# A hybrid mixer and MoE layer: expert weights laid out by groups of 128 rows, contiguous reads on TensorE, routing steps in another order

## The chip, the cores and the metric

The kernel runs on one core of a Trainium2 chip. The metric is the device time of one execution in microseconds (us). The engines are TensorE (PE, with its weight loads as PEld), VectorE (DVE), ScalarE (ACT), GpSimd (POOL) and SyncE (SP); DMA engines, 16 to a core, move data between HBM and SBUF.

## The reference

T = 512 tokens of D = 1024 features, float32. After four token mixers with a gated merge and an output projection (unchanged here) comes a mixture of experts:

```python
def hier_moe(h, wr_g, br_g, wr_e, br_e, w_gate, w_up, w_down):
    '''Top-1 expert group, then top-2 experts inside it; experts are SwiGLU MLPs.'''
    ...
    combine = jnp.sum(jax.nn.one_hot(expert_id, N_EXPERTS, dtype=f32) * top_w[..., None], axis=1)
    hid = jax.nn.silu(jnp.einsum('td,edf->etf', t, w_gate)) * jnp.einsum('td,edf->etf', t, w_up)
    hid = hid * combine.T[:, :, None].astype(hid.dtype)
    out = jnp.einsum('etf,efd->td', hid, w_down)
    ...
        h = h + hier_moe(rms_norm(h, norm2_g[l]), router_w_group[l], ...)
    return rms_norm(h, final_norm_g)
```

There are 16 experts of width 512 in 4 groups; gate and up weights are 1024 x 512 per expert, down weights 512 x 1024.

## The kernel before

The program runs, in this order, the input projection and the mixers, the merge with `w_out` (0 to 617 us with what follows), the routing and the dispatch (about 597 to 616), the 16 experts (616 to 925), and the way back with the last norm (925 to 950). A slot table gives each expert up to 128 tokens.

*Order.* PE's instructions run in the order in which the code issues them (a manual schedule); those of the other engines are ordered by a scheduler from their dependences, and each engine runs its own in order.

*Three passes.* The large matmuls are split into a high and a low part of each operand: ACT copies the high part (L119: `XH`, `nh`, `HH`), DVE subtracts to get the low one (L120: `XL`, `nl`, `HL`), and PE runs three matmuls (L123 to L125). An expert's gate, up and down products (G, U, D) each take four chunks of weights; one chunk is 128 x 1024 elements, feeds six matmuls of 512 columns, and costs one `nh` and one `nl`. `feed` issues these splits ahead into a few slots, which come free when PE has used them.

*Weight loads.* `wload` issues the loads of the expert weights on SP's queue, 1 MB each into one of 13 buffers (named `raw`, `wb`, `m`, `wbx`, `hi`, `lo`, after what lay there). Row r of a weight matrix goes to partition r // 8 for gate and up, and r // 4 for down: 8 KB in one run per partition and load. So partition p holds neighbouring rows, and whatever meets these weights in a matmul has to be read in columns of stride 8 (or 4 for the hidden layer).

*Routing*, for each block t of 128 tokens: `r_t` transposes the activations, `r_mm` (L1072) makes the logits and the norm's factor `rs`, and then DVE's top-k chain, up to `Msel` (one flag per token and expert); `r_h2` scales the activations (`h2`); `r_pos` counts on PE (L1111, L1112), builds the selection `sel` of expert 0 (L1116), and then some 17 small DVE operations of indices and weights; POOL scatters `h2` to `XE` in DRAM by those indices (L1131). `disp` (L1160) gathers expert 0's tokens by a matmul of `h2` and `sel`. The steps of the first three blocks are placed between the matmuls of `w_out`; those of t = 3 stand in a row, as the diff shows.

*Experts.* Expert 0 comes from `disp` directly. The others are loaded from `XE` by POOL's queue (`x_load`, L1272, L1275) and transposed on PE (`xt`, L1234). `h_tr` (L1247) transposes the hidden layer. In experts 0 and 15 U is computed in two halves of 256 columns (`up_halves`), with `h_half` (L1322), so that D can begin sooner. POOL makes index tables for expert 0 (L1294) which PE uses at L1385. At expert 14 POOL makes the tables for the return of experts 14 and 15 (`pT`, L1407), then writes the results of expert 13 to DRAM (L1364) and gathers the earlier results by token (L1372). DVE adds them to what PE returns (L1461, L1463).

Of the kernel before, what the change touches and what calls it, by code (L numbers as in the profile page):

```python
# [1549 lines left out]
```

## Time and profile before

| | |
|---|---|
| median of 3 runs | 951.55 us (951.45 to 951.55) |
| the profiled execution | 951.25 us, span 949.7 us, granted clock 0.99 |
| PE busy | 922.9 us, 97% |
| weight loads (PEld) | 760.1 us, 80% |
| DVE / ACT / POOL busy | 627.8 (66%) / 538.8 (57%) / 101.2 (11%) |
| DMA | 195.7 MB, 206 GB/s over the span |

The span is that of the engines' instructions in the profiled execution; the time of an execution is a little longer. Busy times are sums of records; PE's records overlap, because matmuls are pipelined. Such shares are means over all stages.

### The profile page before, as it was taken

The numbers are of one execution on the slowest core, as the hardware profiler recorded it, in microseconds if no ns is written. First come the engines' busy times: TensorE is split into PE (matmuls) and PEld (weight loads), VectorE is DVE, ScalarE is ACT, GpSimd is POOL, SyncE is SP. The second block draws the span as 40 slices with busy tenths as digits, with TensorE's granted clock in tenths as the row PEclk, the third lists the DMA queues.
The fourth block names the chain that finished last, engine by engine and source line by source line (L and its number), as shares of the span: only waits on it lengthen the run. The fifth ranks groups of instructions, "written<-read, shape, count | busy, mean of one in ns | idle before, by whom it ended". The sixth has DMA issues, their size and how long they took to land. (4 is left out here: it accounts for less than half of the span.)

```text
span 949.7 us, 13038 instructions
## 1 busy us (share of the span) xinstructions
PE 922.9 (97%) x4765; PEld 760.1 (80%) x4765; DVE 627.8 (66%) x1165; ACT 538.8 (57%) x837; POOL 101.2 (11%) x181
## 2 busy tenths in 40 slices
PE   8999999999999999999999999999999999999993
PEld 7979888777768888888888888977888888888882
DVE  6677457888773343444374515658989989999955
ACT  7436548558982232232263314247888888888853
POOL 2000000000000000000000011441110101110750
PEclk9999999999999999999999999999999999999997
DMA  8558456652124224222444437679999999999283
GB/s 246 143 147 283 164 192 222 218 182 89 45 74 129 65 90 131 89 89 89 133 132 163 172 117 288 253 231 332 357 355 397 377 369 382 393 386 380 66 163 110
DMA packets 90047, 195.73 MB, mean 206 GB/s; under 512 B 7388, under 2 KB 63784, under 8 KB 78712
## 3 DMA queue, kind: packets, MB, share of 16 engines
q1 hardware_dynamic: 62312, 153.56, 46.2%
q0 software_dynamic: 6528, 20.29, 7.6%
q10 hardware_dynamic: 21136, 20.98, 6.4%
q8 instruction: 39, 0.64, 0.3%
q14 instruction: 32, 0.26, 0.1%
HBM read 166.24 MB, written 34.60 MB: 211 GB/s over the span
## 5 line engine op out<-in xcount | busy, mean ns | idle before, releaser
L120 DVE TENSOR_TENSOR lo<-raw,hi 128x1024 fp32r<-128x1024 f32 (+3 forms) x70 | 79.0, 1132 | 129.4 <-ACT hi L119 129.1
L119 ACT ACTIVATE hi<-raw 128x1024 fp32r<-128x1024 f32 (+3 forms) x70 | 68.6, 986 | 161.0 <-PE b L124 88.0
L123 PE MATMUL b<-nh,XH 128*128 128x512 f32 (+1 forms) x272 | 109.9, 404 | 0.5 <-ACT XH L119 0.5
L125 PE MATMUL b<-nh,XL 128*128 128x512 f32 (+1 forms) x272 | 108.2, 398 | 0.0
L124 PE MATMUL b<-nl,XH 128*128 128x512 f32 (+1 forms) x272 | 108.1, 397 | 0.0
L123 PE MATMUL b<-nh,hi 128*128 128x512 f32 x256 | 100.1, 391 | 0.0
L124 PE MATMUL b<-nl,hi 128*128 128x512 f32 x256 | 99.8, 390 | 0.0
L125 PE MATMUL b<-nh,lo 128*128 128x512 f32 x256 | 99.7, 389 | 0.0
L123 PE MATMUL mm<-nh,hi 128*128 128x512 f32 x192 | 78.8, 410 | 1.1 <-DVE nl L235 1.1
L125 PE MATMUL mm<-nh,lo 128*128 128x512 f32 x192 | 75.2, 392 | 0.0
L124 PE MATMUL mm<-nl,hi 128*128 128x512 f32 x192 | 75.0, 391 | 0.0
L120 DVE TENSOR_TENSOR nl<-wb,nh 128x1024 fp32r<-128x1024 f32 x56 | 67.2, 1227 | 7.3 <-ACT nh L119 5.2
L120 DVE TENSOR_TENSOR nl<-m,nh 128x1024 fp32r<-128x1024 f32 x56 | 66.9, 1225 | 5.5 <-ACT nh L119 3.5
L120 DVE TENSOR_TENSOR nl<-raw,nh 128x1024 fp32r<-128x1024 f32 x52 | 62.2, 1225 | 7.6 <-ACT nh L119 6.1
L119 ACT ACTIVATE nh<-wb 128x1024 fp32r<-128x1024 f32 x56 | 58.8, 1062 | 13.5 <-PE b L125 8.2
L119 ACT ACTIVATE nh<-m 128x1024 fp32r<-128x1024 f32 x56 | 58.7, 1062 | 11.3 <-PE b L125 8.6
L119 ACT ACTIVATE nh<-raw 128x1024 fp32r<-128x1024 f32 x52 | 54.5, 1062 | 14.0 <-PE b L125 11.2
L125 PEld LDWEIGHTS b<-nh,XL 128*128 128x128 f32 x272 | 52.2, 192 | 12.0 <-DVE XL L120 0.4
L123 PEld LDWEIGHTS b<-nh,XH 128*128 128x128 f32 x272 | 52.4, 193 | 11.4 <-ACT XH L119 0.7
L124 PEld LDWEIGHTS b<-nl,XH 128*128 128x128 f32 x272 | 52.3, 192 | 10.8
L123 PEld LDWEIGHTS b<-nh,hi 128*128 128x128 f32 x256 | 48.0, 188 | 10.4 <-issue 0.2
L124 PEld LDWEIGHTS b<-nl,hi 128*128 128x128 f32 x256 | 48.1, 188 | 10.3 <-issue 0.2
(391 smaller groups left out, 2049.8 us busy)
## 6 DMA issues: line engine op xcount, KB each, us to landing
raw<-in_w_in_dram SPq DMA_DIRECT2D x30, 1024.0 KB, 5.5
XE<-MZ ACTq DMA_DIRECT2D x24, 512.0 KB, 3.8
wb<-in_moe_w_gate_dram SPq DMA_DIRECT2D x10, 1024.0 KB, 8.0
m<-in_moe_w_gate_dram SPq DMA_DIRECT2D x10, 1024.0 KB, 6.2
raw<-in_moe_w_up_dram SPq DMA_DIRECT2D x9, 1024.0 KB, 5.7
wb<-in_moe_w_down_dram SPq DMA_DIRECT2D x9, 1024.0 KB, 5.0
wb<-in_moe_w_up_dram SPq DMA_DIRECT2D x9, 1024.0 KB, 7.1
m<-in_moe_w_up_dram SPq DMA_DIRECT2D x9, 1024.0 KB, 8.3
```

Source lines behind the costliest of these rows:

```text
L119: A.activation(hi, src, AF.Copy)
L120: return V.tensor_tensor(lo, src, hi.bitcast(FT), op=OP.subtract)
L123: PE.matmul(o, w[0], xx[0], start=first, stop=False)
L124: PE.matmul(o, w[0], xx[1], start=False, stop=False)
L125: PE.matmul(o, w[1], xx[0], start=False, stop=last)
```

## The change

Expert weights are loaded so that partition p of group k holds row k·128 + p. Then `disp`, `xt`, `h_tr`, `h_half` and `up_halves` read contiguous columns. The routing steps are cut into smaller ones: `rs` and `h2` come earlier or behind `Msel`, `r_pos` keeps the count and `sel`, and the rest of it becomes `r_idx`, which for t = 2 and 3 is issued behind the last `Msel`. POOL's memsets go, since the first three loads of `X` are whole, and the tables `pT` move to DVE.

```diff
     def wload(ap, h):
...
-        src = ap.rearrange("(p k) f -> p (k f)", p=128)[:, h * 2048:(h + 1) * 2048]
-        n = 2048 // len(ws)
+        n, m = 2048 // len(ws), ap.shape[0] // 256 // len(ws)
+        src = ap.rearrange("(k p) f -> p k f", p=128)
         for i, w in enumerate(ws):
-            S.dma_start(w, src[:, i * n:i * n + n])
+            k = (h * len(ws) + i) * m
+            S.dma_start(w.rearrange("p (k f) -> p k f", k=m), src[:, k:k + m])
...
+        return p
+
+    def r_rs(t):
         s2 = sm("s2", 1)
         V.tensor_tensor(s2, ss2[:, t, 0:1], ss2[:, t, 1:2], op=OP.add)
+        rstd(rs2[:, t:t + 1], s2, D)
+
+    def r_top(t, p):
         r2 = rs2[:, t:t + 1]
-        rstd(r2, s2, D)
...
-        V.tensor_tensor(Msel[t], OH[:, 0], OH[:, 1], op=OP.add)
-        XS[t] = OH, ef, lg, g8, e8
-
-    def r_h2(t):
+        MS[t] = V.tensor_tensor(Msel[t], OH[:, 0], OH[:, 1], op=OP.add).ins
+        o0 = sm("o0", 1)
+        V.tensor_tensor(o0, OH[:, 0, 0:1], OH[:, 1, 0:1], op=OP.add)
+        XS[t] = OH, ef, lg, g8, e8, o0
+
+    def r_h2(t, behind=None):
         h2 = h2b[t]
-        V.scalar_tensor_tensor(h2, x1[:, t], rs2[:, t:t + 1], g2b, op0=OP.mult, op1=OP.mult)
-        XS[t] += (h2,)
...
+        with tc.issue_after(behind) if behind else ExitStack():
+            V.scalar_tensor_tensor(h2, x1[:, t], rs2[:, t:t + 1], g2b, op0=OP.mult, op1=OP.mult)
+        HH2[t] = h2
...
     def r_pos(t):
...
         sel = wop.tile([128, 128], FT, name="sel", bufs=4)
-        o0 = sm("o0", 1)
-        V.tensor_tensor(o0, OH[:, 0, 0:1], OH[:, 1, 0:1], op=OP.add)
         V.tensor_scalar(sel, slot, p[:, 0:1], o0, op0=OP.is_equal, op1=OP.mult)
+        SEL[t] = sel
+
+    def r_idx(t):
+        OH, ef, lg, g8, e8, o0 = XS[t]
+        p, h2 = PP[t], HH2[t]
         po = sm("po", 16)
...
     def disp(t, ks=range(KD)):
-        sel, h2 = XS[t]
-        hv = h2.rearrange("p (q k) -> p k q", k=KD)
+        sel, h2 = SEL[t], HH2[t]
         for k in ks:
-            PE.matmul(x0[k // 4][:, (k % 4) * 128:(k % 4 + 1) * 128], hv[:, k], sel, start=t == 0 and k % 4 == 0, stop=t == NT - 1,
+            PE.matmul(x0[k // 4][:, (k % 4) * 128:(k % 4 + 1) * 128], h2[:, k * 128:(k + 1) * 128], sel, start=t == 0 and k % 4 == 0, stop=t == NT - 1,
...
-        pend = [lambda t=t: r_t(t, 0), no, lambda t=t: r_t(t, 1), no, lambda t=t: (r_mm(t), r_h2(t)), no, no,
-                ] + ([lambda t=t: r_pos(t - 1)] if t else [])
+        pend = [lambda t=t: r_t(t, 0), no, lambda t=t: (r_t(t, 1), r_rs(t)), no,
+                lambda t=t: (r_top(t, r_mm(t)), r_h2(t, MS[t])), no, no,
+                ] + ([lambda t=t: (r_pos(t - 1), r_idx(t - 1))] if t else [])
     r_t(3, 0)
     disp(0, range(4))
     r_t(3, 1)
+    r_rs(3)
+    r_h2(3)
     disp(0, range(4, KD))
-    r_mm(3)
+    r_top(3, r_mm(3))
+    disp(1)
     r_pos(2)
-    r_h2(3)
-    disp(1)
     disp(2)
     r_pos(3)
     disp(3)
+    for t in (2, 3):
+        with tc.issue_after(MS[3]):
+            r_idx(t)
...
     def xt(X, q):
-        Xv = X.rearrange("p (q k) -> p k q", k=KD)
...
-                PE.transpose(p[:, k * 128:(k + 1) * 128], Xv[:, i * 4 + k], ident)
+                c = (i * 4 + k) * 128
+                PE.transpose(p[:, k * 128:(k + 1) * 128], X[:, c:c + 128], ident)
...
     def h_tr(H):
         p = bank()
-        Hv = H.rearrange("p (q k) -> p k q", k=4)
         for k in range(4):
-            PE.transpose(p[:, k * 128:(k + 1) * 128], Hv[:, k], ident)
+            PE.transpose(p[:, k * 128:(k + 1) * 128], H[:, k * 128:(k + 1) * 128], ident)
...
-    for X in Xt[1:]:
-        G.memset(X, 0.0)
...
-        if e == 1:
+        if e <= len(Xt):
             G.dma_start(X, XE[e * CAP:e * CAP + CAP])
...
-            if e in (0, NE - 1):
-                o, i = [v.rearrange(a, s=2, q=128) for v, a in ((H[e], "p (s q c) -> p q s c"),
-                                                                (pgu[k], "p (q s c) -> p q s c"))]
-                A.activation(o, i, AF.Silu)
-            else:
-                A.activation(H[e], pgu[k], AF.Silu)
+            A.activation(H[e], pgu[k], AF.Silu)
...
                 feed(1)
-                g.append([v.rearrange("p k (q s c) -> p k s q c", s=2, c=2) for v in ready.popleft()])
-            up_mm(p[s][:, :256], q[e], [v[:, :, s] for v in g[j]], j)
+                g.append(ready.popleft())
+            up_mm(p[s][:, :256], q[e], [v[:, :, s * 256:s * 256 + 256] for v in g[j]], j)
...
-                G.tensor_scalar(pT[:, t], slot, lz[:, a, 1, i:i + 1], lz[:, a, 0, i:i + 1], op0=OP.is_equal,
+                V.tensor_scalar(pT[:, t], slot, lz[:, a, 1, i:i + 1], lz[:, a, 0, i:i + 1], op0=OP.is_equal,
```

On PE, at the end of the routing, from the logits of t = 3 on. Before (`x_4861` and `x_4862` are the two banks of the dispatch, `Msel_4847` to `Msel_4849` the flags of t = 0 to 2):

```order
L1072 MATMUL b<-wr,lo 128x24 x8
L1111 LDWEIGHTS ones
L1111 MATMUL b<-Msel_4847,ones 128x16
L1111 LDWEIGHTS ones
L1111 MATMUL b<-Msel_4848,ones 128x16
L1112 LDWEIGHTS upper
L1112 MATMUL b<-Msel_4849,upper 128x16
L1160 MATMUL x_4861<-sel,lo 128x128 x4
L1160 MATMUL x_4862<-sel,lo 128x128 x4
```

After:

```order
L1073 MATMUL b<-wr,lo 128x24 x8
L1171 MATMUL x_4861<-sel,lo 128x128 x4
L1171 MATMUL x_4862<-sel,lo 128x128 x4
L1121 LDWEIGHTS ones
L1121 MATMUL b<-Msel_4847,ones 128x16
L1121 LDWEIGHTS ones
L1121 MATMUL b<-Msel_4848,ones 128x16
L1122 LDWEIGHTS upper
L1122 MATMUL b<-Msel_4849,upper 128x16
```

The dispatch of t = 1 now stands ahead of the counts of t = 2; nothing else on PE changes its place.

On DVE, where the logits of t = 3 are used. Before, the logits `lg` of t = 3, `sel` of t = 2, and the top-k chain of t = 3 (`MAX`, `MAX_INDEX`) among the operations of `r_pos(2)`:

```order
L1078 SCALAR_TENSOR_TENSOR lg<-b,rs_4852,br 128x24
L1139 TENSOR_TENSOR idx<-dd,sl 128x2
L1116 TENSOR_SCALAR sel<-slot,b,o_5388 128x128
L1080 MAX g_5365<-lg 128x8
L1118 COPY po<-b 128x16
L1082 MAX_INDEX gi_5367<-g_5365,lg 128x8
L1145 SCALAR_TENSOR_TENSOR wd<-ed,gs 128x1
L1120 TENSOR_TENSOR pm<-OH,po 128x32
L1084 CAST gi<-gi_5367 128x1
```

After, with `h2` of t = 3 (`lo`) as the first row:

```order
L1111 SCALAR_TENSOR_TENSOR lo<-xm,rs_4852,g2b 128x1024
L1142 TENSOR_TENSOR ix<-dd,sl 128x2
L1084 SCALAR_TENSOR_TENSOR lg<-b,rs_4852,br 128x24
L1150 TENSOR_SCALAR dd<-sl 128x2
L1124 TENSOR_SCALAR sel<-slot,b,o_5275 128x128
L1151 TENSOR_TENSOR dd<-dd,ovs 128x2
L1086 MAX g_5368<-lg 128x8
L1152 TENSOR_TENSOR idx<-dd,sl 128x2
L1088 MAX_INDEX gi_5370<-g_5368,lg 128x8
```

The chain of t = 3 is still behind `sel` of t = 2. The operations of `r_pos` (`po`, `pm`, `wd`) have left it; with those of t = 3 they are now 35 rows between `sel` of t = 3 and the first `XL`, of which these are the last:

```order
L1151 TENSOR_TENSOR dd<-dd,ovs 128x2
L1161 TENSOR_TENSOR w__5487<-w__5487,ed 128x1
L1152 TENSOR_TENSOR idx<-dd,sl 128x2
L1162 TENSOR_TENSOR ow<-OH,w__5487 128x32
L120 TENSOR_TENSOR XL_5505<-x_4861,XH_5504 128x512
L120 TENSOR_TENSOR XL_5505<-x_4862,XH_5504 128x512
```

The scatters of t = 2 and 3 take their indices `ix` from there, and `XL`, which the first matmuls of expert 0 need, is behind them.

On POOL, from the norm's factors `rs` on. Before (`XE<-hi,ix` and `XE<-lo,ix` are the scatters of t = 0 to 3, two instructions each):

```order
L208 TENSOR_TENSOR rs_4852<-ms,mh 128x1 x2
L1131 DMA XE<-hi,ix 3072x1024 x2
L208 TENSOR_TENSOR rs_4852<-ms,mh 128x1 x2
L1131 DMA XE<-lo,ix 3072x1024 x2
L1265 MEMSET lo 128x1024
L1131 DMA XE<-hi,ix 3072x1024 x2
L1131 DMA XE<-lo,ix 3072x1024 x2
L1265 MEMSET hi 128x1024
L1294 TENSOR_SCALAR lo<-slot,pcs 128x128 x8
```

After (L1307 are the index tables, L1294 before):

```order
L208 TENSOR_TENSOR rs_4852<-ms,mh 128x1 x3
L1144 DMA XE<-hi,ix 3072x1024 x2
L1307 TENSOR_SCALAR lo<-slot,pcs 128x128 x2
L208 TENSOR_TENSOR rs_4852<-ms,mh 128x1
L1307 TENSOR_SCALAR lo<-slot,pcs 128x128 x2
L1144 DMA XE<-lo,ix 3072x1024 x2
L1307 TENSOR_SCALAR lo<-slot,pcs 128x128 x4
L1144 DMA XE<-hi,ix 3072x1024 x2
L1144 DMA XE<-lo,ix 3072x1024 x2
```

The memsets are gone and the tables stand ahead of the scatters of t = 2 and 3.

## Rows read from the trace of the kernel before

**Rows 1.** The page: PE's busy time, and the largest group of `nl` (busy us, mean ns | idle before, releaser).

```profile
PE 922.9 (97%) x4765; PEld 760.1 (80%) x4765; DVE 627.8 (66%) x1165; ACT 538.8 (57%) x837; POOL 101.2 (11%) x181
...
L120 DVE TENSOR_TENSOR nl<-wb,nh 128x1024 fp32r<-128x1024 f32 x56 | 67.2, 1227 | 7.3 <-ACT nh L119 5.2
```

**Rows 2.** Busy time by stretch: the stretch and its length, then busy us (instructions) of PE, PEld, DVE, ACT and POOL, PE's granted clock, the share of the DMA engines, GB/s.

```profile
680.00:740.00 60.00, 60.00 (x283) 49.27 (x282) 55.06 (x54) 51.26 (x61) 7.04 (x26) 1.00 1.02 383
...
870.00:907.60 37.60, 37.60 (x175) 30.74 (x174) 33.46 (x32) 32.15 (x38) 21.27 (x18) 1.00 0.39 133
```

**Rows 3.** Timeline of PE around a contiguous group of 128x128 matmuls (L604), and in the dispatch: start us, length us, line, operation, tiles, count, and in brackets an idle time and what ended it.

```profile
178.21 1.95 PE L604 MATMUL mm<-w,yb 128*128 128x128 f32 x16
179.99 0.60 PE L827 MATMUL at<-ident,t 128*128 128x128 f32 x4
...
597.56 2.07 PE L1160 MATMUL x<-sel,hi 128*128 128x128 f32 x8
599.46 0.60 PE L1062 MATMUL b<-ident,xm 128*128 128x128 f32 x4
...
601.79 1.86 PE L1072 MATMUL b<-wr,lo 128*128 128x24 f32 x16
...
611.99 4.18 PE L1160 MATMUL x<-sel,lo 128*128 128x128 f32 x16 [0.45 <-DVE sel L1116]
...
616.97 0.40 PE L125 MATMUL b<-nh,XL 128*128 128x512 f32 x1
```

**Rows 4.** Groups by line and shape, whole span: busy us, mean ns | idle before.

```profile
L1160 PEld LDWEIGHTS x<-sel,lo 128*128 128x128 f32 x32 | 7.8, 335 | 0.5 <-DVE sel L1116 0.5
...
L604 PEld LDWEIGHTS mm<-w,yb 128*128 128x128 f32 x32 | 4.0, 191 | 0.2
...
L818 DVE TENSOR_SCALAR t<-t,sm 128x128 f32<-128x128 f32 x16 | 3.9, 284 | 0.2
```

**Rows 5.** Timeline of PE at the halves of experts 0 and 15: the first row of each (L123, 128x256) and the first of the down projection behind it.

```profile
626.05 0.46 PE L123 MATMUL b<-nh,XH 128*128 128x256 f32 x1
...
637.31 0.50 PE L123 MATMUL x<-nh,HH 128*128 128x512 f32 x1
...
907.66 0.39 PE L123 MATMUL b<-nh,XH 128*128 128x256 f32 x1
...
918.88 0.50 PE L123 MATMUL x<-nh,HH 128*128 128x512 f32 x1
```

**Rows 6.** Timeline of PE, contiguous matmuls of 256 columns: the first and the last of fifteen.

```profile
75.90 0.28 PE L568 MATMUL mm<-hi,nh 128*128 128x256 f32 x1
...
77.58 0.28 PE L568 MATMUL mm<-lo,nh 128*128 128x256 f32 x1
```

**Rows 7.** Timeline of PE, one `h_tr` and what follows.

```profile
661.57 0.63 PE L1247 MATMUL b<-ident,H 128*128 128x128 f32 x4
661.95 0.48 PE L123 MATMUL b<-nh,XH 128*128 128x512 f32 x1
```

**Rows 8.** Timeline of DVE in the routing of t = 2 and 3.

```profile
603.92 1.22 DVE L1116 TENSOR_SCALAR sel<-slot,b,o 128x128 f32<-128x128 f32 x1
...
605.20 0.09 DVE L1082 MATCH_VALUE_LOAD gi<-g,lg 128x8 f32 x1
...
607.25 0.16 DVE L1097 TENSOR_TENSOR Msel<-OH 128x16 bf16<-128x16 f32 x1
...
611.85 0.17 DVE L1118 COPY po<-b 128x16 f32<-128x16 f32 x1
...
613.84 0.16 DVE L1139 TENSOR_TENSOR idx<-dd,sl 128x2 int32<-128x2 f32 x1
```

**Rows 9.** Timeline of POOL: memset, tables, first load of X.

```profile
604.09 0.97 POOL L1265 MEMSET lo<- 128x1024 f32 x1
...
616.74 5.97 POOL L1294 TENSOR_SCALAR lo<-slot,pcs 128x128 f32<-128x128 f32 x4
...
625.71 0.63 POOL L1272 DMA_DIRECT2D hi<-XE  x1
```

**Rows 10.** Timeline of PE at the table matmuls.

```profile
622.10 1.06 PE L1385 MATMUL b<-ow,lo 128*128 128x16 f32 x8
624.07 0.40 PE L1385 MATMUL b<-ow,lo 128*128 128x16 f32 x2 [0.91 <-POOL lo L1294]
```

**Rows 11.** DMA issues of the page: KB each, median us from issue to landing.

```profile
m<-in_moe_w_up_dram SPq DMA_DIRECT2D x9, 1024.0 KB, 8.3
```

**Rows 12.** Timeline of POOL (return tables) and of DVE (first add of the return).

```profile
893.23 6.38 POOL L1407 TENSOR_SCALAR hi<-slot,lz 128x128 f32<-128x128 f32 x2
...
929.68 1.28 DVE L1463 TENSOR_TENSOR xm<-xm,b 128x512 f32<-128x512 f32 x2 [2.64 <-PE b L1461]
```

**Rows 13.** Busy time by stretch, columns as in rows 2: a long stretch with loads of `w_in` (runs of 1 KB) and `w_branch` (2 KB), one load of `w_branch` alone, one load of expert weights alone.

```profile
280.00:340.00 60.00, 60.00 (x268) 48.92 (x263) 21.45 (x23) 17.17 (x22) 0.00 (x0) 1.00 0.34 107
...
333.90:337.40 3.50, 3.50 (x18) 2.86 (x17) 0.32 (x1) 1.42 (x2) 0.00 (x0) 1.00 0.81 298
...
581.60:585.20 3.60, 3.60 (x22) 3.01 (x21) 2.20 (x8) 1.81 (x4) 0.55 (x1) 1.00 0.77 278
```

**Rows 14.** Timeline of SP (two loads of up weights) and of ACT (the first split of one of them).

```profile
814.29 2.60 SPq L1018 DMA_DIRECT2D m<-in_moe_w_up_dram  x2
...
849.24 1.07 ACT L119 ACTIVATE nh<-m 128x1024 fp32r<-128x1024 f32 x1
```

More of the change, by code (lines that the diff above doesn't have):

```diff
@@ L1054, in wo_mm @@
         sumsq(ss2[:, t, hf:hf + 1], xs, jk)
-    XS = {}
+    XS, MS = {}, {}
     def r_t(t, q):
@@ L1096, in r_mm @@
                         op=OP.is_equal)
-        V.tensor_tensor(Msel[t], OH[:, 0], OH[:, 1], op=OP.add)
-        XS[t] = OH, ef, lg, g8, e8
-    def r_h2(t):
+        MS[t] = V.tensor_tensor(Msel[t], OH[:, 0], OH[:, 1], op=OP.add).ins
[3 more added lines that the diff above has]
+    def r_h2(t, behind=None):
         h2 = h2b[t]
-        V.scalar_tensor_tensor(h2, x1[:, t], rs2[:, t:t + 1], g2b, op0=OP.mult, op1=OP.mult)
-        XS[t] += (h2,)
-    scat = []
+        with tc.issue_after(behind) if behind else ExitStack():
+            V.scalar_tensor_tensor(h2, x1[:, t], rs2[:, t:t + 1], g2b, op0=OP.mult, op1=OP.mult)
+        HH2[t] = h2
+    scat, HH2, SEL, PP = [], {}, {}, {}
     def r_pos(t):
-        OH, ef, lg, g8, e8, h2 = XS[t]
-        p = bank()
+        OH, ef, lg, g8, e8, o0 = XS[t]
+        p = PP[t] = bank()
         for tt in range(t):
@@ L1113, in r_pos @@
         sel = wop.tile([128, 128], FT, name="sel", bufs=4)
-        o0 = sm("o0", 1)
-        V.tensor_tensor(o0, OH[:, 0, 0:1], OH[:, 1, 0:1], op=OP.add)
         V.tensor_scalar(sel, slot, p[:, 0:1], o0, op0=OP.is_equal, op1=OP.mult)
+        SEL[t] = sel
+    def r_idx(t):
+        OH, ef, lg, g8, e8, o0 = XS[t]
+        p, h2 = PP[t], HH2[t]
         po = sm("po", 16)
@@ L1151, in r_pos @@
         V.tensor_copy(lz[:, t, 1], po[:, NE - 2:])
-        XS[t] = sel, h2
     x0 = [bank("x0", 2), bank("x0", 2)]
     def disp(t, ks=range(KD)):
-        sel, h2 = XS[t]
-        hv = h2.rearrange("p (q k) -> p k q", k=KD)
+        sel, h2 = SEL[t], HH2[t]
         for k in ks:
-            PE.matmul(x0[k // 4][:, (k % 4) * 128:(k % 4 + 1) * 128], hv[:, k], sel, start=t == 0 and k % 4 == 0, stop=t == NT - 1,
+            PE.matmul(x0[k // 4][:, (k % 4) * 128:(k % 4 + 1) * 128], h2[:, k * 128:(k + 1) * 128], sel, start=t == 0 and k % 4 == 0, stop=t == NT - 1,
                       skip_group_check=True)
@@ L1310, in run_up @@
             H[e] = Ht[e % 2]
-            if e in (0, NE - 1):
-                o, i = [v.rearrange(a, s=2, q=128) for v, a in ((H[e], "p (s q c) -> p q s c"),
-                                                                (pgu[k], "p (q s c) -> p q s c"))]
-                A.activation(o, i, AF.Silu)
-            else:
-                A.activation(H[e], pgu[k], AF.Silu)
+            A.activation(H[e], pgu[k], AF.Silu)
     def h_half(e, s):
         p = bank()
-        Hv = H[e][:, s * 256:s * 256 + 256].rearrange("p (q c) -> p c q", c=2)
         for c in range(2):
-            PE.transpose(p[:, c * 128:(c + 1) * 128], Hv[:, c], ident)
+            PE.transpose(p[:, c * 128:(c + 1) * 128], H[e][:, s * 256 + c * 128:s * 256 + c * 128 + 128], ident)
         o = [v[:, 2 * s:2 * s + 2].rearrange("p k t -> p (k t)") for v in HQ]
```

## The prediction

> **What bounds the kernel now.** I read the page's totals first: PE is busy 97% of a span of 949.7 us [rows 1]. So a gain has to come out of PE's own instructions, or out of one of its few waits. The table by stretches says who is next: from 680 to 740 us PE is busy all the time at a granted clock of 1.00 (the higher of its two levels, 2.4 GHz), DVE 92% of it, ACT 85%, and the DMA engines show a share above one [rows 2]. PE is first there, but DVE and the weight loads stand close behind it.
>
> Records of PE overlap, so I cost PE by the distance from one start to the next, not by mean durations. Read in that way the timeline shows two places where the same work is dear. Eight dispatch matmuls take 1.90 us (597.56 to 599.46), 238 ns each; sixteen contiguous ones of the same shape 1.78 us (178.21 to 179.99), 111 ns [rows 3]. The weight load of the dispatch matmul, which reads every eighth column, takes 335 ns against 191 [rows 4]. The halves of the up projection of experts 0 and 15 read two columns of every four: 48 matmuls and two transposes take 11.26 us (626.05 to 637.31), 229 ns each when 0.28 goes to the transposes [rows 5]; fifteen contiguous 256-column matmuls stand 120 ns apart (75.90 to 77.58) [rows 6]. The transposes of h_tr, though strided too, are not dear: four take 0.38 us [rows 7].
>
> **The change, part by part.** The profiled execution took 951.25 us, 0.3 below the median of the runs and 1.55 above its span; the sum goes against 951.25.
>
> *Dispatch and routing.* 64 matmuls × (238 − 111) ns is 8.1 us of PE work [rows 3]. Not all of it can arrive, because DVE's chain stands behind it. Step by step: the 16 matmuls of disp(0) ahead of r_mm(3) give 2.0 us, so r_mm(3), from 601.8 now, ends at about 601.5; its logits follow at 601.9, since h2(3), as wide as nl (1.23 us [rows 1]), is now ahead of them on DVE. disp(1) runs from 601.5 to 603.3 ahead of the counts of t=2; then comes sel(2), which took 1.22 us beside POOL's memset [rows 8, 9] and takes some 0.3 without it (the nearest form has 284 ns [rows 4]). Behind it on DVE stands the top-k chain of t=3, 2.2 us from the row at 605.20 to the end of Msel [rows 8]; so Msel(3) comes at about 606.1, while PE, having ended disp(2) at 605.6, waits. sel(3) at 606.6, disp(3) from 606.7 to 608.5; it started at 611.99 [rows 3]. What is late next is XL: 35 small operations of r_idx(2) and r_idx(3) stand ahead of it on DVE. Where they are independent one comes every 79 ns (605.20 to 607.25, 27 rows), in one chain every 142 (611.85 to 613.84, 15 rows) [rows 8]: 2.8 to 5.0 us from 606.6. With 0.7 us for XL, half as wide as nl, the first matmul that needs it starts between 610.1 and 612.3, against 616.97 [rows 3]. Gain 4.7 to 6.9. POOL's tables now run beside these operations and can stretch them as the memset stretched sel, so I take 5.3, and keep 3.5 as the lower bound.
>
> *Index tables of expert 0.* The matmuls at L1385 take 3.95 us (622.10 to 626.05), most of it in waits for POOL [rows 5, 10]. POOL began the tables at 616.74, behind the last scatter [rows 9]. Now the memsets are gone and the tables stand ahead of the scatters of t=2 and 3: done at about 613, before G0 ends at 616.8. Sixteen matmuls at 111 ns are 1.8 us: gain 2.15, at least 1. The price is that the last scatters, and so x_load(1), stand behind them; still it goes out at some 617 where it went out at 625.71 [rows 9], and if it lands as late as a weight load, in 8.3 us [rows 11], it is there before D0 starts (637.31 less 12 us).
>
> *Halves of experts 0 and 15.* 11.26 and 11.22 us [rows 5] become 48 × 120 ns and 0.3 for the transposes, 6.1: a gain of 5.2 each. But four chunks of weights are split in this time, and nl takes DVE 1.23 us a chunk [rows 1], so the chunks of D0 and D15 come later against PE than before. Half a microsecond each is given back: 4.7 + 4.7. The bounds are 5.2 each, and 3.2 if two are given back.
>
> *Transposes.* h_tr's 0.38 us for four is 95 ns each, less than the 111 of contiguous matmuls [rows 3, 7]: little is left to gain. 176 transposes × 0 to 5 ns: I take 0.4, bounds 0 and 0.9.
>
> *Return tables.* Eight 128x128 operations move to DVE: 284 ns each by the nearest row of that form, 2.3 us in all [rows 4]. DVE is busy 33.46 of 37.6 us there [rows 2], which covers them but for moments when a chunk has little lead: 0.3 lost, bounds 0 and 2.3. POOL is rid of them (they last until 899.61 [rows 12]), and the writes of Y13 and the gathers, which stand behind them, start sooner. This is needed: the adds of the return waited for PE, not for the gathers (2.64 us at 929.68 [rows 12]), but PE arrives 17 us sooner now.
>
> *Weights in 128-row groups.* A load of 1 MB is now in runs of 2 KB (gate, up) or 4 KB (down) rather than 8 KB. Lone loads: w_branch, in 2 KB runs, moves 298 GB/s, expert weights in 8 KB runs 278 [rows 13]. So no loss by these. Against that, a long stretch with runs of 1 and 2 KB gives 107 GB/s at a share of 0.34, 315 per full share, and the expert stretch 383 at 1.02, or 375 [rows 2, 13]: up to 19% longer. 1 MB at 383 GB/s is 2.7 us; six loads per expert would take 0 to 3.1 us more. The cover is the lead of the loads: one issued at 814.29 is used at 849.24 [rows 14] and lands in 8.3 [rows 11], so 27 us early. Over 13 experts that lasts up to 2.1 us each. I take a third of the upper price, 1 us each (nearer to the lone loads, which show it directly), and so nothing on the path.
>
> Sum: 5.3 + 2.15 + 4.7 + 4.7 + 0.4 − 0.3 = 16.95; 951.25 − 16.95 = **934.3 us**.
>
> **One rule weighed.** The rows show that reading two columns of every four nearly doubles the distance, 229 against 120 ns [rows 5, 6]. The Trainium skill, page "SBUF — State Buffer", section "Specifications (TRN2)", says that SBUF has lines of 16 bytes and that two hits in a line are enough for full bandwidth. By that rule the two float32 columns taken from each line of the halves cost nothing, and the 229 ns have another cause; by the rows it is the stride. The sum would be 934.3 by the rows and 943.7 by the rule.
>
> **The rivals.**
> - *The halves keep their pace*: two adjacent columns are enough, and something else makes these matmuls 229 ns. Then both terms of 4.7 fall: 943.7. Against it: shape and type are those of the 120 ns rows [rows 6]. The rule above stands for it.
> - *DVE and POOL take the gain back*: 3.5 for the dispatch, 1 for the tables, 3.2 for each pair of halves, nothing for the transposes, 1 lost to the return tables: 9.9, so 941.3. For it: DVE's 92% [rows 2], and sel's 1.22 us beside POOL [rows 8].
> - *The dispatch is slow for another reason than its stride*: only waits are saved there, about 1: 938.6. Against it: the weight load of 335 ns [rows 4]. For it: the transposes, strided too, pay almost nothing [rows 7].
> - *All comes through*: 6.9, 2.15, 5.2, 5.2, 0.9 and no loss: 930.9.
> - *Slower*: the DMA engines become the bound from about 700 us on, where they have nothing idle [rows 2]. The point from which they delay PE at all is 2.1 us per expert, where the lead runs out; to be slower than before they must eat the 16.95 too: (27 + 16.95)/13 = 3.4 us per expert, 21% on six loads of 2.7 us. That is just above the upper price of 19%. At 25%: 4.05 × 13 − 27 − 16.95 = 8.7 more than before, 960.0.
>
> **How the numbers follow.** The forecast (931 to 938) gets 0.66; all through 0.08; DVE and POOL 0.12 (938 to 942); the dispatch 0.04; the halves 0.04; the DMA engines 0.06, of which 0.04 is slower. The range 929.5 to 942.5 reaches a little below the sum of all gains, and leaves out the halves, the DMA engines and an edge of DVE and POOL, under 0.2. Within 0.2% (1.9 us, about what a measurement of this kernel can tell from no change) I put 0.02, faster 0.94, slower 0.04.
>
> **What would show it.** Right: sixteen dispatch matmuls from start to start in about 1.8 us, with a weight load near 191 ns; the halves of expert 0 and of expert 15 in about 6; the table matmuls in 1.8 without a wait; no PE or ACT wait on a weight load. Wrong: dispatch matmuls still 238 apart, halves at 229, PE, ACT or DVE waiting for a DMA of wload, or the adds of the return waiting for the gathers. The first waits that I expect to see are PE's on sel(3) and on XL.

## The result, and the profile after

The changed kernel takes **936.84 us** (median of 4 runs, 936.31 to 938.37) where the kernel before takes 951.55 (4 runs, 951.45 to 953.21): a ratio of 0.9844, 95% interval 0.9827 to 0.9861. That is 14.7 us faster. The forecast was 934.3, with a range of 929.5 to 942.5. The execution profiled here, the slowest of the four, took 938.37 us, 1.8 more than its span. Of the experiments below, one of four executions of `rs_first` took 3796.53 us, for a reason that no trace shows; it is left out of the ratio given there as a slow one.

The page of the changed kernel: span and totals, and one of the loads (KB, us to landing).

```profile
span 936.6 us, 13010 instructions
...
PE 906.4 (97%) x4765; PEld 741.8 (79%) x4765; DVE 628.0 (67%) x1173; ACT 538.6 (58%) x837; POOL 82.1 (9%) x165
...
m<-in_moe_w_up_dram SPq DMA_DIRECT2D x9, 1024.0 KB, 10.3
```

PE has the same 4765 matmuls and 16.5 us less busy time, still at 97%: the time came out of PE's own instructions [rows 1]. POOL is 19 us lighter; DVE is unchanged. The loads land later than before (10.3 where [rows 11] has 8.3).

The timeline of PE in the changed kernel, from the dispatch to the second half of expert 0, and from the half of expert 15 to the end of the expert:

```profile
600.09 1.06 PE L1171 MATMUL x<-sel,hi 128*128 128x128 f32 x8
600.98 0.60 PE L1063 MATMUL b<-ident,xm 128*128 128x128 f32 x4
...
608.18 2.05 PE L1171 MATMUL x<-sel,hi 128*128 128x128 f32 x16 [2.08 <-DVE dd L1151]
...
611.43 2.05 PE L1171 MATMUL x<-sel,lo 128*128 128x128 f32 x16 [0.61 <-DVE sel L1124]
613.32 0.25 PE L1218 MATMUL b<-Msel,ones 128*128 128x16 bf16 x4
...
615.15 0.50 PE L125 MATMUL b<-nh,XL 128*128 128x512 f32 x1 [0.31 <-DVE XL L120]
...
620.39 1.86 PE L1392 MATMUL b<-ow,lo 128*128 128x16 f32 x16
622.10 0.37 PE L123 MATMUL b<-nh,XH 128*128 128x256 f32 x1
...
628.95 0.50 PE L123 MATMUL x<-nh,HH 128*128 128x512 f32 x1 [0.60 <-ACT HH L119]
...
898.55 0.28 PE L123 MATMUL b<-nh,XH 128*128 128x256 f32 x1
...
902.17 0.38 PE L124 MATMUL b<-nl,XH 128*128 128x256 f32 x1 [0.62 <-DVE nl L120]
...
906.05 0.50 PE L123 MATMUL x<-nh,HH 128*128 128x512 f32 x1 [0.76 <-ACT HH L119]
```

Eight dispatch matmuls take 0.89 us (600.09 to 600.98) where they took 1.90 [rows 3]; the sixteen table matmuls run in 1.71 us without a wait, where the stage took 3.95 [rows 5, 10]; the halves take 6.85 and 7.50 us where they took 11.26 and 11.22 [rows 5]. New is a wait of 2.08 us in the dispatch. The weight loads by shape (busy us, mean ns | idle before) say the same of the stationary reads: 192 ns where [rows 4] has 335, and 141 and 140 for the transposes of X and H, which had 192 and 203.

```profile
L1171 PEld LDWEIGHTS x<-sel,lo 128*128 128x128 f32 x32 | 3.7, 192 | 1.2 <-DVE sel L1124 1.2
...
L1250 PEld LDWEIGHTS b<-ident,hi 128*128 128x128 f32 x80 | 9.3, 141 | 1.4 <-DMA hi<-XE 0.2
...
L1262 PEld LDWEIGHTS b<-ident,H 128*128 128x128 f32 x56 | 7.0, 140 | 2.0
```

The same transposes before:

```profile
L1234 PEld LDWEIGHTS b<-ident,hi 128*128 128x128 f32 x80 | 10.5, 192 | 0.9
...
L1247 PEld LDWEIGHTS b<-ident,H 128*128 128x128 f32 x56 | 8.9, 203 | 1.2
```

Taken apart by PE's starts in the two profiles, us:

| stage | before | after | difference | forecast |
|---|---|---|---|---|
| ahead of `r_t(3)` (L1062/L1063) | 597.09 | 599.61 | +2.5 | 0 |
| dispatch, up to the table matmuls | 25.01 | 20.78 | −4.2 | −5.3 |
| table matmuls | 3.95 | 1.71 | −2.2 | −2.15 |
| halves of expert 0 and its down projection | 18.66 | 13.94 | −4.7 | −4.7 |
| experts 1 to 14 | 238.30 | 237.52 | −0.8 | −0.4 |
| stage with the return tables | 24.65 | 24.99 | +0.3 | +0.3 |
| halves of expert 15 and its down projection | 17.71 | 13.67 | −4.0 | −4.7 |
| tail | 24.3 | 24.4 | 0.0 | 0 |
| sum | 949.7 | 936.6 | −13.1 | −16.95 |

Two differences are to be explained: 1.1 us in the dispatch, and 2.5 ahead of `r_t(3)`. Most of the second comes and goes. 1.6 of it lies in one place, shown here in the profile of the changed kernel (stretch and length, busy us and instructions of PE, PEld, DVE, ACT, POOL, PE's granted clock, DMA share, GB/s):

```profile
279.00:280.20 1.20, 0.43 (x6) 0.43 (x8) 1.00 (x2) 0.72 (x2) 0.00 (x0) 0.94 0.00 0
280.20:281.40 1.20, 1.20 (x14) 0.92 (x10) 0.00 (x0) 0.00 (x0) 0.00 (x0) 0.50 0.00 0
281.40:282.50 1.10, 1.10 (x4) 0.54 (x3) 0.00 (x0) 0.00 (x0) 0.00 (x0) 0.50 0.00 0
...
680.00:740.00 60.00, 60.00 (x278) 48.74 (x277) 54.61 (x53) 51.68 (x61) 8.54 (x28) 1.00 1.04 369
```

and in another profiled execution of the same kernel, of 936.00 us (`same_chip_after` below):

```profile
280.20:281.40 1.20, 1.20 (x9) 0.56 (x4) 0.00 (x0) 0.00 (x0) 0.00 (x0) 1.00 0.00 0
```

PE waited 1.30 us for ACT up to 279.8; behind that wait its granted clock was 0.50 (1.2 GHz) for some 3.3 us (280.1 to 283.4) in the one execution, and 1.00 (2.4 GHz) throughout in the other, as in the profile of before. Five of the fourteen profiles of this document have the low clock there. The execution without it has a span of 934.3 us and reaches `r_t(3)` at 597.56, so 15.4 us less than before in span, with 0.5 of the 2.5 left.

Of that half microsecond, 0.4 belongs to the change, whose new order of steps begins with the first three blocks of the routing, between the matmuls of `w_out`. From the matmul behind the wait of 1.30 us to `r_t(3)`, all seven profiles with the new order and the full clock take 318.20 to 318.22 us; before and `layout_only` below, with the old order, take 317.84 and 317.83; the five with the low clock take 319.79 to 319.84. What the change does is therefore seen best from `r_t(3)` to the end of the span: 352.6 us before, 337.0 and 336.7 in the two profiles of the changed kernel, so 15.6 to 15.9 less.

### The profile page after: what moved, and what is told of

Read it like the earlier page. It is cut to its first block, busy times and chain, and to the rows that moved or that the text cites. A ratio compares the mean times of both kernels' runs of the same rounds, so it can differ in the third digit from the quotient of the medians.

```text
span 936.6 us, 13010 instructions
## 1 busy us (share of the span) xinstructions
PE 906.4 (97%) x4765; PEld 741.8 (79%) x4765; DVE 628.0 (67%) x1173; ACT 538.6 (58%) x837; POOL 82.1 (9%) x165
## 5 line engine op out<-in xcount | busy, mean ns | idle before, releaser
L123 PE MATMUL b<-nh,XH 128*128 128x512 f32 (+1 forms) x272 | 105.5, 388 | 1.1 <-ACT XH L119 1.1
L124 PE MATMUL b<-nl,XH 128*128 128x512 f32 (+1 forms) x272 | 103.8, 382 | 0.6 <-DVE nl L120 0.6
L125 PE MATMUL b<-nh,XL 128*128 128x512 f32 (+1 forms) x272 | 104.0, 382 | 0.3 <-DVE XL L120 0.3
L123 PE MATMUL b<-nh,hi 128*128 128x512 f32 x256 | 100.5, 393 | 0.0
L123 PE MATMUL mm<-nh,hi 128*128 128x512 f32 x192 | 78.8, 410 | 1.1 <-DVE nl L235 1.1
L123 PEld LDWEIGHTS b<-nh,XH 128*128 128x128 f32 x272 | 51.1, 188 | 11.6 <-ACT XH L119 1.4
L123 PEld LDWEIGHTS b<-nh,hi 128*128 128x128 f32 x256 | 48.2, 188 | 10.7 <-issue 0.5
## 6 DMA issues: line engine op xcount, KB each, us to landing
m<-in_moe_w_up_dram SPq DMA_DIRECT2D x9, 1024.0 KB, 10.3
```

The costliest lines, as they stand in the source:

```text
L123: PE.matmul(o, w[0], xx[0], start=first, stop=False)
L124: PE.matmul(o, w[0], xx[1], start=False, stop=False)
L125: PE.matmul(o, w[1], xx[0], start=False, stop=last)
```

## The experiments

**What is PE's new wait in the dispatch?** The timeline of POOL in the changed kernel:

```profile
604.37 1.21 POOL L1307 TENSOR_SCALAR lo<-slot,pcs 128x128 f32<-128x128 f32 x2 [4.43 <-PE b L1073]
605.56 0.57 POOL L208 TENSOR_TENSOR rs<-ms,mh 128x1 f32<-128x1 f32 x1
...
628.59 0.59 POOL L1285 DMA_DIRECT2D hi<-XE  x1 [7.37 <-DMA XE<-lo,ix]
```

and of DVE:

```profile
606.16 1.41 DVE L1111 SCALAR_TENSOR_TENSOR lo<-xm,rs,g2b 128x1024 f32<-128x1024 f32 x1 [2.55 <-POOL rs L208]
...
607.78 0.34 DVE L1124 TENSOR_SCALAR sel<-slot,b,o 128x128 f32<-128x128 f32 x1
```

The row of PE's wait names `dd`, which ended beside sel(2); the other profile of the same kernel has the wait with sel itself as its end:

```profile
606.12 2.05 PE L1171 MATMUL x<-sel,hi 128*128 128x128 f32 x16 [2.08 <-DVE sel L1124]
```

The tables (L1307) go into the buffer `lo`, which `r_mm(3)` reads, so they wait for PE (4.43 us). `rs(3)`, one column wide, stands behind two of them on POOL; `h2(3)` (L1111) waits 2.55 us for `rs(3)`; and sel(2), for which PE waits, stands behind `h2(3)` on DVE. The first experiment issues the tables behind `rs(3)`:

```
-        G.tensor_tensor(dst, m[:, :w], mh[:, :w], op=OP.pow)
+        return G.tensor_tensor(dst, m[:, :w], mh[:, :w], op=OP.pow)
...
-        rstd(rs2[:, t:t + 1], s2, D)
+        MS['rs'] = rstd(rs2[:, t:t + 1], s2, D).ins
...
-        G.tensor_scalar(ph[:, i], slot, pcs[:, i // 2, i % 2:i % 2 + 1], None, op0=OP.is_equal)
+        with tc.issue_after(MS['rs']):
+            G.tensor_scalar(ph[:, i], slot, pcs[:, i // 2, i % 2:i % 2 + 1], None, op0=OP.is_equal)
```

> The changed kernel, with the eight index tables issued behind the norm's factor rs of t = 3 on POOL. Queue theory: rs(3) is late (605.56) only because two tables stand ahead of it, and they wait for the logits r_mm(3), whose input lies in the buffer that the tables overwrite. Then rs(3) comes before 603, h2(3) no longer holds up sel(2), PE's wait of 2.08 us ahead of the dispatch of t = 2 goes, and disp(3) starts 1.5 to 2.1 us sooner: the kernel is 1.5 to 2.1 us faster than the changed one. Rival, DVE's own chain: top-k, which stands behind sel(2), sets the start of disp(3) anyway; then at most 0.3 us is gained and the wait moves to sel of t = 3.

Measured: 934.66, 934.95 and 936.79 us, ratio 0.9835 (0.9815 to 0.9855). Its timeline of PE:

```profile
604.56 2.05 PE L1171 MATMUL x<-sel,hi 128*128 128x128 f32 x16 [0.46 <-DVE sel L1124]
...
609.25 0.25 PE L1218 MATMUL b<-Msel,ones 128*128 128x16 bf16 x4
```

The wait is 0.46 instead of 2.08, and the dispatch ends 11.64 us after `r_t(3)` (597.61) instead of 13.71. The cause of this wait is shown. What arrives of it was measured with both kernels on one chip, five runs each:

> The changed kernel as it is, on the chip and among the runs of the next two kernels. Expected: 935.5 to 938.5 us in the single runs, since its profile has about 2 us that come and go ahead of the stage of the change (the granted clock at 0.50 behind one wait at 280 us). If those 2 us are an accident of single executions, some of these runs lie near 935 and others near 938; if the changed kernel always has them, all lie together.

> The same computation, POOL's index tables issued behind rs(3). The queue theory (PE's 2.08 us wait for sel(2) is DVE's h2(3) waiting for rs(3) behind two tables on POOL) expects 1.5 to 2.1 us less than the changed kernel on this chip, comparing medians of runs taken in turn. The rival, that the time saved there is given back at the halves of expert 0 or at the X load of expert 1 (which already landed only just in time), expects 0 to 0.7 less.

Measured: 936.88 us (936.00 to 937.25) against 934.79 (934.53 to 934.88); ratios to before 0.9844 (0.9830 to 0.9857) and 0.9821 (0.9807 to 0.9834). By the medians that is 2.1 us less, and all five runs lie below all five of the changed kernel. In the two profiles, neither of which has the low clock at 280 us, the spans are 934.3 and 933.1: 1.2 us, and 1.1 of it is there at the first half of expert 0 (the first row is of the changed kernel, the second of the other; each starts from `r_t(3)` at 597.56 and 597.59).

```profile
619.87 0.36 PE L123 MATMUL b<-nh,XH 128*128 128x256 f32 x1
```

```profile
618.75 0.36 PE L123 MATMUL b<-nh,XH 128*128 128x256 f32 x1
```

At the end of the dispatch the lead is 1.7 (611.09 and 609.44): 0.5 is given back on the way to the halves. The other 0.9 us of the medians may be the clock at 280 us: three of the five runs of the changed kernel (936.88 to 937.25) had a mean granted clock of 0.991 to 0.992, two (936.00 and 936.36) 0.994. Only the profiled run shows where, so this part is argued. From `r_t(3)` to the end, the two profiles of the edit have 335.3 and 335.5 us, so 1.2 to 1.7 less than the changed kernel's.

**Is it the stride that made the dispatch dear?** The changed kernel with the old read of h2:

```
-            PE.matmul(..., h2[:, k * 128:(k + 1) * 128], sel, ...)
+            PE.matmul(..., h2.rearrange("p (q k) -> p k q", k=KD)[:, k], sel, ...)
```

> The changed kernel, with the dispatch alone reading every eighth column again (the weights stay in groups of 128 rows, so expert 0 gets its rows in another order than its weights; only the time is of use). Stride theory: weight loads of 335 ns and 238 to 244 ns from start to start return, 8.1 us of PE work, of which the waits ahead of disp(2) and disp(3) (2.08 + 0.36 + 0.61 us) and the one on XL hide three to four: 4 to 5 us slower than the changed kernel. Rival, the stride costs nothing and the dispatch was slow for another reason: 111 ns stays, no change.

Measured: 943.47 us (941.48 to 943.85), ratio 0.9908 (0.9891 to 0.9924), 6.6 above the changed kernel. In its timeline sixteen matmuls take 3.96 us (605.70 to 609.66, where the next begins); the changed kernel has 1.87 (604.01 to 605.88):

```profile
605.70 4.16 PE L1171 MATMUL x<-sel,lo 128*128 128x128 f32 x16
610.39 4.19 PE L1171 MATMUL x<-sel,hi 128*128 128x128 f32 x16 [0.46 <-DVE sel L1124]
```

and its weight loads, by shape:

```profile
L1171 PEld LDWEIGHTS x<-sel,lo 128*128 128x128 f32 x32 | 7.8, 334 | 0.6 <-DVE sel L1124 0.6
```

The stride is the cause, and costs more than expected: `r_t(3)` to the end of the dispatch takes 19.81 us instead of 13.71. PE's waits in it fall from 3.05 us to 0.92, and nothing else hides the slower reads. From `r_t(3)` to the end of the span the profile has 5.8 to 6.1 us more than those of the changed kernel; the rest of the 6.6 lies ahead of it, where this profile too has the low clock.

**What makes the halves dear?** First the changed kernel with two columns of every four again, then expert 0 with four of every eight and expert 15 with one of every two:

```
-            up_mm(p[s][:, :256], q[e], [v[:, :, s * 256:s * 256 + 256] for v in g[j]], j)
+            c = ...   # 2; then 4 for expert 0 and 1 for expert 15
+            up_mm(p[s][:, :256], q[e], [v.rearrange("p k (q s c) -> p k s q c", s=2, c=c)[:, :, s] for v in g[j]], j)
```

> The changed kernel, with the halves of experts 0 and 15 reading two columns of every four again (which columns belong to which half then no longer fits the hidden layer; only the time is of use). Stride theory: 229 ns from start to start, 48 x 109 ns = 5.2 us more for each expert, less what the waits behind the halves hide now (0.60 us at D0; 0.62 and 0.76 at expert 15): 4 to 4.7 us each, 8 to 9.4 together. Rule theory (two hits in a line of 16 bytes are enough): 120 ns stays, no change.

> The changed kernel, with the halves reading pieces: expert 0 four columns of every eight, expert 15 one column of every two (the halves then don't fit the hidden layer; only the time is of use). Line theory (a line of 16 bytes is four float32 columns; a line that is used in full costs nothing, one used in part costs its whole time): expert 0 stays at 120 ns from start to start, expert 15 goes to about 229. Span theory (the read passes over what it skips, or pays at each break): both go to about 229. Rule theory in its plain form (two hits in a line are enough): 120 and, with two of four columns of each line hit, 120.

Measured: 945.62 us (945.19 to 946.06), ratio 0.9938 (0.9921 to 0.9954), 8.8 above the changed kernel; and a single run of 942.04. The second one's timeline of PE:

```profile
621.67 0.36 PE L123 MATMUL b<-nh,XH 128*128 128x256 f32 x1
...
628.50 0.51 PE L123 MATMUL x<-nh,HH 128*128 128x512 f32 x1 [0.60 <-ACT HH L119]
...
898.08 0.39 PE L123 MATMUL b<-nh,XH 128*128 128x256 f32 x1
...
909.30 0.50 PE L123 MATMUL x<-nh,HH 128*128 128x512 f32 x1
```

Four of eight columns cost 6.83 us, as contiguous ones do (6.85); one of two costs 11.22, as two of four did [rows 5]. In these stretches the granted clock is 1.00. So it is not the jump as such: pieces of 16 bytes that are read whole are free here, pieces of which half is read take about twice the time, whether that half is one stretch or two. Other shares of 16 bytes were not tried. The rule weighed in the prediction, of the Trainium skill ("SBUF — State Buffer", section "Specifications (TRN2)"), has lines of 16 bytes and asks for at least two hits in a line for full bandwidth; the same row of that page adds a penalty for each cross to a new line, which the prediction left out. The trace fits lines of 16 bytes; that two hits are enough it does not bear out for these matmuls, 229 ns against 120.

**What does the reordering bring by itself?** The kernel before with the new layout and contiguous reads alone (routing order, memsets and return tables on POOL as before):

```
-        src = ap.rearrange("(p k) f -> p (k f)", p=128)[:, h * 2048:(h + 1) * 2048]
+        src = ap.rearrange("(k p) f -> p k f", p=128)
-            PE.matmul(..., hv[:, k], sel, ...)
+            PE.matmul(..., h2[:, k * 128:(k + 1) * 128], sel, ...)
```

> The kernel before with the weights in groups of 128 rows and all reads contiguous, but its own order of routing steps, its memsets and tables on POOL. Theory that the new order of steps gives little by itself: without h2(3) and the tables in front, disp(3) ends about 2.8 us sooner than in the changed kernel, but the tables of expert 0 end late behind memset and scatters and PE waits for them 3 to 4 us; 1 to 3 us slower than the changed kernel. Rival, the new order brings most of the gain of the dispatch: 4 to 6 us slower, with the dispatch itself longer.

Measured: 938.95 us (938.83 to 939.36), ratio 0.9869 (0.9852 to 0.9885): 12.6 of the 14.7 us, leaving 2.1 for all the rest. From `r_t(3)` to the end of the span it is 12.4 of the 15.6 to 15.9, leaving 3.3 to 3.5. Its timelines of POOL and of PE:

```profile
610.36 0.95 POOL L1263 MEMSET hi<- 128x1024 f32 x1 [0.17 <-issue]
611.30 6.19 POOL L1292 TENSOR_SCALAR lo<-slot,pcs 128x128 f32<-128x128 f32 x3
```

```profile
619.29 1.77 PE L1377 MATMUL b<-ow,lo 128*128 128x16 f32 x6 [0.18 <-POOL lo L1292]
620.90 0.56 PE L123 MATMUL b<-nh,XH 128*128 128x256 f32 x1
621.26 0.41 PE L124 MATMUL b<-nl,XH 128*128 128x256 f32 x1
...
621.90 0.41 PE L124 MATMUL b<-nl,XH 128*128 128x256 f32 x1
```

Its dispatch is over 11.24 us after `r_t(3)` (597.06 to 608.30), 2.5 sooner than in the changed kernel; but its table matmuls take 5.88 us (615.02 to 620.90), waiting for POOL. The waits for the tables cost a second time: behind them the granted clock is 0.50 up to 626, the contiguous matmuls of the halves stand 213 ns apart (three from 621.26 to 621.90), and the halves of expert 0 take 9.14 us (620.90 to 630.04) instead of 6.85. So the new order buys the tables (4.2 us) and the clock behind them (2.3) with the dispatch (2.5), through the queue on POOL.

**Must the return tables leave POOL?** The changed kernel with the tables back on POOL (`V.tensor_scalar(pT[:, t], ...)` becomes `G.tensor_scalar`). The edit moves all eight, where the expectations here and below say seven:

> The same computation as the changed kernel, but with seven of the eight return tables back on POOL. The prediction's theory (POOL must be rid of them, or the gathers of the return come late now that PE arrives sooner) expects the adds of the return to wait for the gathers and 1 us or more lost. The rival (there is slack of several us between the gathers and the adds; DVE pays 272 ns each for the tables, hidden but for some 0.3) expects the adds to wait for PE as before and the time unchanged to 0.4 us less.

Measured: 935.77 us (935.36 to 937.39), ratio 0.9834 (0.9821 to 0.9848), 1.1 below the changed kernel on the same chip by medians, with intervals that overlap. Its timelines of POOL (seven of the tables, and the last gather of the return) and of DVE (the first add, and that of t = 3):

```profile
873.41 12.16 POOL L1414 TENSOR_SCALAR hi<-slot,lz 128x128 f32<-128x128 f32 x7 [9.25 <-PE b L1250]
...
907.22 2.28 POOL L1379 DMA_INDIRECT xm<-YE,idx  x1 [0.66 <-DMA xm<-YE,idx]
```

```profile
915.64 1.28 DVE L1470 TENSOR_TENSOR xm<-xm,b 128x512 f32<-128x512 f32 x2 [2.64 <-PE b L1468]
...
923.38 1.28 DVE L1470 TENSOR_TENSOR xm<-xm,b 128x512 f32<-128x512 f32 x2
```

The last gather, for t = 3, is issued 5 us later than in the changed kernel (902.41). The one landing that the trace has took 9.6 us, and the DMA engines fall idle at about 917 (share 0.42 at 916.0 to 916.5, 0.09 in the next half microsecond). The add that needs this gather starts at 923.38, so some 6 us of slack are left. The first add, at 915.64, waits for PE, 2.64 us, the same as before [rows 12]. The stage with the tables takes 24.59 us; in both profiles of the changed kernel 24.99 and 24.97, before 24.65. So the move to DVE costs 0.4 us and buys nothing here. From `r_t(3)` to the end the profile has 0.3 to 0.6 less than those of the changed kernel; the rest of the 1.1 the profiles do not show.

**Do shorter runs of the loads cost?** The changed kernel with runs of 8 KB, and with runs of 1 KB, by the source address alone:

```
-        src = ap.rearrange("(k p) f -> p k f", p=128)
+        src = ap.rearrange("(p k) f -> p (k f)", p=128)[:, h * 2048:(h + 1) * 2048]     # 8 KB
...
+        ap.rearrange("k (a b) -> (k a) b", b=256).rearrange("(k p) b -> p k b", p=128)   # 1 KB
```

> The changed kernel, with the weights loaded in runs of 8 KB per partition as before, while all reads stay contiguous (the rows of the weights then don't fit those of the activations; only the time is of use). Cover theory: the landings of the weight loads, 7.3 to 13.2 us in the changed kernel, go back to the 5.0 to 8.8 of before, PE has no wait more or less, and the time is within 0.7 us of the changed kernel. Rival, the longer loads cost something that no wait shows (traffic that slows the X loads and the scatters): 1 us or more faster.

> The changed kernel, with the weights loaded in runs of 1 KB (four, or eight, rows of a quarter width per partition: the weights are then in another order; only the time is of use). DMA theory: the engines are full, runs of 1 KB take 19% longer than the mix of before (315 against 375 GB/s per full share), 3 us per expert, so the lead of 25 us is used up by about the ninth expert and PE waits for weights at the end: landings over 30 us, 8 to 15 us slower than the changed kernel. Rival, the engines keep their rate with runs of 1 KB: landings up by less than 5 us, no wait of PE, no change.

Measured with 8 KB: 938.11 us (937.65 to 942.31), ratio 0.9854 (0.9838 to 0.9871): 1.3 above the changed kernel, which neither theory expected. Its timelines of POOL and PE:

```profile
630.69 0.59 POOL L1284 DMA_DIRECT2D hi<-XE  x1 [8.66 <-DMA XE<-lo,ix]
```

```profile
639.32 1.97 PE L1249 MATMUL b<-ident,hi 128*128 128x128 f32 x8 [2.47 <-DMA hi<-XE]
```

The weights land sooner (6.2 to 10.0 us), but the X load of expert 1 goes out later (its wait for the scatters is 8.66 instead of 7.37), and PE waits 2.47 us for it. That longer runs hold up the scatters on their way is a guess from one profile, that of the slowest of the five executions (942.31, with `r_t(3)` at 600.58); whether the others have the wait is not shown.

With 1 KB a single run took 958.18 us, 21 above. The windows (columns as above), and ACT's waits:

```profile
680.00:740.00 60.00, 60.00 (x278) 48.76 (x277) 54.72 (x53) 51.34 (x60) 8.54 (x28) 1.00 1.09 337
```

```profile
906.83 1.06 ACT L119 ACTIVATE nh<-raw 128x1024 fp32r<-128x1024 f32 x1 [9.71 <-DMA raw<-in_moe_w_up_dram]
...
920.29 2.00 ACT L119 ACTIVATE nh<-wbx 128x1024 fp32r<-128x1024 f32 x2 [10.30 <-DMA wbx<-in_moe_w_down_dram]
```

337 GB/s at a share of 1.09 is 309 per full share, near the 315 of the stretch of 1 and 2 KB runs before [rows 13]; the changed kernel has 369 at 1.04, 355. The time from the issue of a load to its first use falls over the experts: for the buffer `wbx` it is 31.9 us at first (669.62 to 701.57) and 13.4 at 859.69, where the changed kernel keeps some 35. PE stays busy all the time up to 860, and starves only at the end. The mechanism of the slower rival is real; runs of 2 and 4 KB lie on its safe side. All this is from a single run.

**A faster version.** Two more kernels build on the first experiment: one (`best2`) issues the weights half of `r_idx(2)` and `r_idx(3)` behind XL, and in the halves issues a product on DVE ahead of the next splits; the other has the first experiment's edit and the return tables on POOL.

> rs_first, and the weights of the routing (the second half of r_idx) for t = 2 and 3 issued behind XL, so that 26 small operations instead of 35 or more stand ahead of XL and of the scatters' indices. Queue theory: XL of expert 0 and so G0 come 0.8 to 1.3 us sooner than in rs_first; but the first load of X, which waits for the scatters to land, holds the transposes of expert 1 (0.20 us already in rs_first), so of it 0.3 to 0.8 us reaches the end: 934 to 935 by the median. Rival: DVE's work is only moved, between the splits of G0's weights, and PE waits there instead: no gain over rs_first.

> The same computation as the changed kernel, with both edits that gained: the index tables behind rs(3) on POOL, and seven of the eight return tables on POOL. If the two gains add up, since they lie 260 us apart: 1.2 to 1.5 us less for the first and 0.4 less for the second, so 934.2 to 934.5 us where the kernel with the first alone has 934.8. If the gathers of the return, which now have 6 us less lead, come into the way: 934.8 or more, and the adds of the return wait for them.

Measured: 934.57 us (934.29 to 936.35), ratio 0.9825 (0.9809 to 0.9841); and 934.84 (934.30 to 936.32), ratio 0.9827 (0.9814 to 0.9840). Neither can be told from 934.79. In the first, PE still waits for XL, 1.19 us. Between sel(3) and XL stand 20 operations where `rs_first` has 32, yet XL starts at 610.47 against 610.59: the operations left take up to 0.64 us each there, where POOL runs four tables beside them (608.22 to 610.58).

```profile
611.21 0.50 PE L125 MATMUL b<-nh,XL 128*128 128x512 f32 x1 [1.19 <-DVE XL L120]
```

In the second the stage with the tables has its 24.58 us, but another wait has grown in the timeline of PE:

```profile
632.93 1.09 PE L1250 MATMUL b<-ident,hi 128*128 128x128 f32 x8 [0.71 <-DMA hi<-XE]
```

The X load of expert 1 is now close to the bound of this stage: PE waits for it 0.71 us here and 0.20 in `rs_first`, and not in the profiles of `same_chip_rs_first` and `best2`. Issuing the tables behind `rs(3)` is the edit that beats both kernels, 16.8 us under before.

## Why the prediction was right, point by point

- *What bounds the kernel, and the price of the strides*: right. The strided dispatch and halves were the cost, 12.6 of 14.7 us by the layout alone, and the strides put back took 6.6 and 8.8 us. Two rivals fell, that the halves keep their pace and that the dispatch is slow for another reason. The sum did not come right by luck: against the forecast 1.1 us are missing in the dispatch and 0.7 at expert 15, 0.4 came in addition from experts 1 to 14, and the largest miss is the start (2.5 in the profiled execution).
- *Halves, 4.7 each*: 4.7 and 4.0. The half microsecond set aside for chunks that come late through DVE is seen at expert 0 as PE's 0.60 us for HH, so in another place: HH stands on ACT behind the split `nh` of a chunk (627.59 to 628.63). At expert 15, beside 0.76 for HH, there is a second wait, 0.62 for `nl`, behind 1.4 us of expert 14's results (L1363) on DVE; no experiment took these apart.
- *Tables, 2.15*: 2.2.
- *Dispatch, 5.3*: 4.2, the mis-sized term. The step that failed is the chain on DVE: "sel(2)" was taken to follow `h2(3)` with that one ready, and sel(3) and XL were named as the first waits. But `h2(3)` had to wait for `rs(3)`, behind two tables on POOL, and PE waited 2.08 us for sel(2); sel itself took 0.34, as forecast, and the waits for sel(3) and XL were 0.61 and 0.31. POOL's order in the document ahead of the prediction shows the tables; what was not asked is from when they could run and what stood behind. With the tables behind `rs(3)`, `r_t(3)` to the halves takes 21.16 us (597.59 to 618.75), where the forecast had 28.96 − 5.3 − 2.15 = 21.5.
- *The X load of expert 1 out at 617*: wrong, it went out at 628.59, because it waits 7.37 us for the last scatters to land. It was counted to land before the down projection of expert 0 began; with the shorter dispatch of the last experiment PE waits for it, 0.71 us.
- *Transposes, 0.4*: 0.8 over experts 1 to 14, inside the bound of 0.9.
- *Return tables, 0.3 lost*: 0.3 to 0.4. That POOL had to be rid of them was wrong: some 6 us of slack remain with them on POOL. The adds' wait for PE was read rightly, but what the gathers could still give was not subtracted.
- *Loads, nothing on the path*: right. By the medians of the page the loads of 1 MB land in 7.3 to 13.2 us where they landed in 5.0 to 8.8, and so use some 3 us of about 27 of lead. PE waits for no weight load; ACT waits for one, 0.34 us at 757.6.
- *Start*: 0.5 to 2.5 us were lost ahead of `r_t(3)`, which no step spoke of: 0.4 by the new order of steps in the first three blocks, the rest by what comes and goes.

## What to carry to other kernels

Cost a strided operand by rows of the same stride, by whether it uses each 16 bytes whole, and by whether the engine has anything to hide it: here a layout fixed once by the order of the load removed the price of every later read. When work is moved ahead in a queue, ask of each moved instruction from when it can run and which short instruction of another chain then stands behind it: a one-column operation behind two tables cost 1 to 2 us of 5. Look at the granted clock behind a wait of PE, too: in `layout_only` the 4.2 us lost at the tables cost another 2.3 behind them. And when an early stage gets shorter, look at the loads that start from its end, for they don't get shorter with it.

## What the runs showed of the hardware

- TensorE's moving read: 256 columns take 120 ns when each 16 bytes read are used whole (contiguous, or four of eight float32) and about twice that when half is used (two of four: 229 ns [rows 5]; one of two: 11.22 us for the same 48 matmuls and two transposes). A stationary 128x128 float32 tile takes 335 ns at every eighth column and 192 contiguous in the dispatch; in the transposes 192 and 141.
- At a granted clock of 0.50 the contiguous 256 columns take 213 ns (`layout_only`), and two of every four, before, 227 (nine matmuls from 628.15 to 630.19) against 230 at 1.00 (thirteen from 632.24 to 635.23): the lower clock adds nothing to the half-used read.
- The granted clock fell to 0.50 behind the same wait of 1.30 us in five profiles and not in nine, and cost 1.6 us where it did.
- With the DMA engines full (three stretches from 680 us on in each profile), runs of 1 KB move 309 to 316 GB/s per full share, runs of 2 and 4 KB 355 to 367, and before, in 8 KB, 363 to 384 (375 in [rows 2]).
- A 128x128 return table costs some 270 ns on DVE (seven in 1.88 us from 876.09) and 1.7 us on POOL while DVE runs its splits (seven in 12.16 us). An index table took POOL 0.6 us with DVE idle (two in 1.21 us at 604.37) and also beside DVE's small operations (four in 2.41 at 611.81), and 2.1 in the mean beside splits (three in 6.19, `layout_only`).
